# Layer 1's projections ahead of its attention, and one PSUM bank for a head's scores and transposes

## The chip, the cores and the metric

One core of a Trainium2 chip runs the whole program: two transformer blocks of two layers each, on 256 tokens (and 256 context tokens in the first block), width 1024, batch 1, float32. The metric is the device time of one execution in microseconds, as the median of several. Three executions of the kernel before took 2139.5, 2148.2 and 2151.42 us, so the median is 2148.2 us.

## The reference, cut to what matters

Only the attention of the first block is touched. Its layer 0 holds the MLA attention (`blocked_attention`, 8 heads, 512 tokens of context and latent for queries, 256 or 512 keys). Its layer 1 is `odd_mixer`:

```python
lat = split_cols(u_lat @ w_in, ODD_SPLITS); ctx = split_cols(u_ctx @ w_in, ODD_SPLITS)
c_lat = neighbourhood_attention(q0, k0, v0, k_ctx, v_ctx, rpb)   # 8 heads of 64: softmax(q k^T * s + bias) v
kd_c = rms_norm(k of ctx);  kd_l = apply_rope(rms_norm(k));  qd_l = apply_rope(rms_norm(q))
d_lat = blocked_attention(qd_l, concat(kd_c, kd_l), concat(vd_c, vd_l), scale)   # 8 heads, 2 KV heads
y_lat = concat(c_lat, d_lat) @ w_out
```

## The kernel before, in words

A matrix product in float32 is made of three matmuls on split operands (`mm3`, lines 554 to 556): each operand is a high part and a rest. Weights come by DMA on SP's queue in groups of two 128-row tiles (`Weights.load`), ACT casts the high part (L270) and DVE or POOL subtracts for the rest (L272). `linear_tok` runs over (chunk of columns, token tile) in an order given by the caller, loads a chunk's four groups at its first tile, and hands each finished PSUM bank to `consume`. In layer 1 the weights have two pools: the common one (2 raw, 2 split buffers) and `K.px` (1 raw, 2 split); `layer1` closes `K.px` after the mixer and opens a larger one for `w_out`.

The Tile framework orders the instructions: program order is the priority, and in a simulated time line each engine takes the ready instruction of highest priority, so that later code fills holes of earlier code. On the chip each engine then runs its list in that fixed order.

PSUM has eight banks of 128x512 float32. In layers 1 to 3 `mix_banks` names them acc (2), aux (1), s (2), tp (2), po (1). In layer 0 they are g (3), s (2), tp (1), po (1), gv (1), where acc is another name of s and aux of g.

`attend` treats a pair of heads for one tile of 128 queries: six score matmuls (two heads, three steps, L710) into two banks; for each head the negated maximum on DVE (L674), exp with its sum on ACT (L676), four PE transposes of the 128x512 result (L679) into another bank, a copy to SBUF (head 0 on ACT, L684; head 1 on DVE, L682). Then the reciprocal of the sums (L698), its transpose into `rb` (L700), and 16 matmuls with v into `po` (L690). Tiles p and pt have K.np = 2 buffers each. The list `kinds` says which bank each score and each transposed tile gets. `attended` (L718, L719 and a split, L306, L307) closes four pairs of a token tile.

`l1_mixer` runs: projections of v, k, q (chunks 2, 1, 0); neighbourhood attention `na(0)` on token tile 0, whose scores get a bias by DMA on POOL's queue (L1406) and a DVE add (L1407); projections of the grouped attention (chunks 4, 3), with per-head norm and rope; `na(1)`; the transposes put off into `late` (four of k, two of q, all through the one aux bank, L1350); `gqa(0)`, `gqa(1)`. There are 16 calls of `attend`. After it comes the `w_out` product.

In layer 0 `l0_mla` calls `attend` 16 times, beside the delta rule's recurrence (`gdn_run`) for head pairs 0 and 1 and after it for pairs 2 and 3. Rotary tables for the second block (`rope2_tables`) use DVE and ACT inside layer 1's attention.

Of the kernel before, what the change touches and what calls it, by code (L numbers as in the profile page):

```python
# [163 lines left out]
def closed(K, p):  # L164
    for q, cm in K.open:
        if q is p:
            cm.__exit__(None, None, None)
# [32 lines left out]
def bank(K, kind):  # L200
    kind = K.alias.get(kind, kind)
    return K.ps[kind].tile([128, 512], F32, name=nm(K, kind), tag=kind, bufs=K.kinds[kind])
# [459 lines left out]

def attend(K, score, v, po, rb, c, kinds=("s", "s", "tp", "tp")):


    nc = K.nc
    sm = cut(K, [128, 2], F32, "sm", 4)
    pts = []  # L670
    for hh, ps in enumerate(score([bank(K, kinds[0]), bank(K, kinds[1])])):
        n = ps.shape[-1]
        nmx = cut(K, [128, 1], F32, "nmx", 6)
        nc.vector.tensor_reduce(nmx, ps, axis=AX.X, op=ALU.max, negate=True)  # L674
        p = cut(K, [128, 512], F32, "p", K.np)
        nc.scalar.activation(p[:, :n], ps, AF.Exp, bias=nmx, accum_out=sm[:, hh:hh + 1])  # L676
        tp = bank(K, kinds[2 + hh])
        for j in range(n // 128):
            nc.tensor.transpose(tp[:, j * 128:(j + 1) * 128], p[:, j * 128:(j + 1) * 128], K.ident)  # L679
        pt = cut(K, [128, 512], F32, "pt", K.np)  # L680
        if hh:
            nc.vector.tensor_copy(pt[:, :n], tp[:, :n])  # L682
        else:
            nc.scalar.copy(pt[:, :n], tp[:, :n])  # L684
        pts.append((pt, n // 128))
    sums_row(K, sm.unsqueeze(1), rb, c)
    nj = pts[0][1]
    for j in range(nj):
        for hh in range(2):
            nc.tensor.matmul(po[hh * 64:hh * 64 + 64, c:c + 128], v(hh, j), pts[hh][0][:, j * 128:(j + 1) * 128],  # L690
                             start=(j == 0), stop=(j == nj - 1))
# [96 lines left out]
def l0_mla(K, O):  # L788

    nc = K.nc  # L790
# [7 lines left out]
    for t in range(4):  # L798
        n = vt[:, t, :]
# [17 lines left out]
    for k in range(4):  # L817
        ps = acc(K)
# [7 lines left out]
        g = K.col("mla_qn")[:, k:k + 1] if k < 2 else K.col("mla_kvn")  # L826
# [6 lines left out]
    for t in range(4):  # L833
        ps = acc(K)
# [4 lines left out]
    for pair in range(4):  # L839
        heads = {}  # L840
        for h in (2 * pair, 2 * pair + 1):
            if h % 4 == 0:
                wq = WQ.load(K.ins["w_q"], 0, 2, (h // 4) * 512, 512)
            late = "g" if pair >= 2 else None
            ps = bank(K, late or "acc")
            hs = slice((h % 4) * 128, (h % 4 + 1) * 128)
            for k in range(2):
                mm3(K, ps, wq[0][:, k, hs], wq[1][:, k, hs], qh[:, k, :], ql[:, k, :], k == 0, k == 1)
            u = cut(K, [128, 512], F32, "p", K.np)
            nc.vector.tensor_tensor(u, ps, K.c("qtab"), op=ALU.mult)  # L850
            q1, q2 = cut(K, [128, 512], FR, "q1", 2), cut(K, [128, 512], FR, "q2", 2)
            split(K, q1, q2, u)
            ps = bank(K, late or "acc")
            hs = slice(h * 64, (h + 1) * 64)
            mm3(K, ps[:64, :], wkh[:, 0, hs], wkl[:, 0, hs], ch, cl, True, True)
            k1, k2 = kh[h % 2], kl[h % 2]
            nc.scalar.copy(k1[:64, :], ps[:64, :])
            nc.vector.tensor_tensor(k2[:64, :], ps[:64, :], k1.bitcast(F32)[:64, :], op=ALU.subtract)
            heads[h] = (q1, q2, k1, k2)
        po, rb = bank(K, "po"), bank(K, "gv")  # L860
        for t in range(4):
            n = 256 if t < 2 else 512

            def score(pss):
                tk = slice(t * 128, (t + 1) * 128)
                for hh in range(2):
                    q1, q2, k1, k2 = heads[2 * pair + hh]
                    mm3(K, pss[hh][:, :n], q1[:, tk], q2[:, tk], k1[:, :n], k2[:, :n], True, True)
                    yield pss[hh][:, :n]
            attend(K, score, lambda hh, j: vt[:, j, pair * 128 + hh * 64:pair * 128 + hh * 64 + 64], po, rb, t * 128,  # L870
                   ("s", "g", "tp", "g") if late else ("s", "s", "tp", "tp"))
        nc.scalar.copy(O[:, pair, :], rb)
        nc.vector.tensor_tensor(O[:, pair, :], po, O[:, pair, :], op=ALU.mult)

# [479 lines left out]
def l1_mixer(K, W, oh, ol):  # L1354

    nc = K.nc
    w = K.ins["w_in_odd"][0]
    xs = kts(K.uh, K.ul)
    kh, kl = cut(K, [128, 4, 512], FR), cut(K, [128, 4, 512], FR)
    qh, ql = cut(K, [128, 4, 256], FR), cut(K, [128, 4, 256], FR)  # L1360
    gkh, gkl = cut(K, [128, 2, 512], FR), cut(K, [128, 2, 512], FR)
    gqh, gql = cut(K, [128, 4, 256], FR), cut(K, [128, 4, 256], FR)
    vn, vg = cut(K, [128, 4, 512]), cut(K, [128, 4, 128])
    rt = K.c("rope_gqa").rearrange("p (t c) -> p t c", t=2)

    def tok(t):
        return slice(t * 128, (t + 1) * 128)

    def consume(ci, t, ps):
        if ci == 2:  # L1370
            nc.scalar.copy(vn[:, t, :], ps)
            return
        x = cut(K, [128, 512], F32, "lx", 3) if ci < 3 else cut(K, [128, 512 if ci == 3 else 256], F32, "lx%d" % ci, 2)
        if ci == 4:
            nc.scalar.copy(x[:, :256], ps[:, :256])
            nc.gpsimd.tensor_copy(vg[:, t, :], x[:, 128:256])
            xv = x[:, :128].rearrange("p (h d) -> p h d", h=2)
            per_head_norm(K, xv, 2, K.row("gqa_kn"))
            if t >= 2:
                rope_tok(K, xv, 2, 64, rt[:, t - 2, :64], rt[:, t - 2, 64:], nc.gpsimd, "rk")  # L1380
            kd = cut(K, [128, 2, 2, 64], F32, "lkd", 4)
            nc.vector.tensor_copy(kd, bc(xv, [128, 2, 2, 64], 2))
            late.append(lambda: pairs_T(K, kd.rearrange("p g x d -> p (g x d)"), 2, gkh, gkl, tok(t)))
            return
        nc.scalar.copy(x, ps)
        if ci == 0:
            pairs_T(K, x, 4, qh, ql, tok(t - 2), 0.125)
        elif ci == 1:
            pairs_T(K, x, 4, kh, kl, tok(t))
        else:  # L1390
            xv = x.rearrange("p (h d) -> p h d", h=8)
            per_head_norm(K, xv, 8, K.row("gqa_qn"))
            rope_tok(K, xv, 8, 64, rt[:, t - 2, :64], rt[:, t - 2, 64:], nc.gpsimd, "rq")
            late.append(lambda: pairs_T(K, x, 4, gqh, gql, tok(t - 2), 0.125))

    chunks = [(0, 512), (512, 512), (1024, 512), (1536, 512), (2048, 256)]
    late = []

    def na(t):
        po, rb = bank(K, "po"), aux(K)  # L1400
        for pair in range(4):
            def score(pss):
                out = pair_scores(K, (qh[:, pair], ql[:, pair]), (kh[:, pair], kl[:, pair]), 512, tok(t), pss)
                for hh in range(2):
                    b = cut(K, [128, 256], F32, "nab", 4)
                    nc.gpsimd.dma_start(b, K.ins["rpbx"][2 * pair + hh, t * 128:(t + 1) * 128, :])  # L1406
                    nc.vector.tensor_tensor(out[hh][:, 256:], out[hh][:, 256:], b, op=ALU.add)  # L1407
                return out
            attend(K, score, lambda hh, j: vn[:, j, pair * 128 + hh * 64:pair * 128 + hh * 64 + 64], po, rb, pair * 128,
                   ("s", "acc", "tp", "acc") if t == 1 and pair >= 1 else ("s", "s", "tp", "tp"))  # L1410
        attended(K, po, rb, oh, ol, 0, t)

    def gqa(t):
        po, rb = bank(K, "po"), aux(K)
        for pair in range(4):
            g = pair // 2

            def score(pss):
                return pair_scores(K, (gqh[:, pair], gql[:, pair]), (gkh[:, g], gkl[:, g]), 512, tok(t), pss)
            attend(K, score, lambda hh, j: vg[:, j, g * 64:g * 64 + 64], po, rb, pair * 128, ("s", "acc", "tp", "acc"))  # L1420
        attended(K, po, rb, oh, ol, 4, t)

    linear_tok(K, W, xs, w, chunks, [(2, 0), (2, 1), (2, 2), (2, 3), (1, 0), (1, 1), (1, 2), (1, 3), (0, 2), (0, 3)],
               consume)
    na(0)
    linear_tok(K, W, xs, w, chunks, [(4, t) for t in range(4)] + [(3, 2), (3, 3)], consume)
    na(1)
    for f in late:
        f()
    for t in range(2):  # L1430
        gqa(t)

# [524 lines left out]
def layer1(K, h):  # L1959
# [5 lines left out]
    with Pool(K, "l1o"):  # L1965
# [5 lines left out]
        bk = ffn_banks(K)  # L1971
        bk.__enter__()
        K.dbg("oh", oh)
        closed(K, K.px)
        W.drop()
        pa = opened(K, "a", "right")
        K.uh, K.ul = sbt(K, [128, 8, 256], FR, pool=pa), sbt(K, [128, 8, 256], FR, pool=pa)
        K.pa = pa
# [192 lines left out]
```

## Time and profile before

| | |
|---|---|
| executions, us | 2139.5, 2148.2, 2151.42 |
| profiled execution, us | 2141.66 |
| its span in the trace, us | 2139.8 |
| PE busy, DVE busy, ACT busy, us | 2003.9, 1318.1, 923.5 |
| first projection matmul of layer 1 to its first w_out matmul, us of the span | 908.2 to 1104.9 |

The span is the time from the first to the last instruction of the profiled execution; the execution itself is 1.86 us longer. A busy share is the share of a stretch in which an engine ran an instruction. The clock column of a stretch (PEclk) is the mean granted clock of TensorE as a share of 2.4 GHz: 1.00 is the full clock and 0.50 the lower level of 1.2 GHz. Layer 1's mixer is the stretch from 908 to 1105 us, layer 0's MLA attention runs from 302 to 440 us.

### The profile page before, as it was taken

The page shows a single profiled execution, that of the slowest core. Times are in us where ns is not written, and L with a number is a line of the kernel's source. Part 1 is how long each engine was busy: PE and PEld are TensorE (multiplying, and loading weights), DVE is VectorE, ACT ScalarE, POOL GpSimd, SP SyncE. Part 2 cuts the span into 40 slices and gives each one's busy share as a digit, 9 for nine tenths or more (in the row PEclk, how much of TensorE's full clock was granted, in tenths as well). Part 3 has the DMA queues.
Part 4 walks back from the last instruction along what each step waited for, and adds up shares of the span by engine and source line. Part 5 has one row for each costly group of instructions (what it writes and reads, how often), then busy time and mean ns, then how long its engine had stood idle before and what let it go on. Part 6 is the DMA issues. An engine that isn't in the chain of part 4 may idle for free.

```text
span 2139.8 us, 31171 instructions
## 1 busy us (share of the span) xinstructions
PE 2003.9 (94%) x11656; PEld 1629.7 (76%) x11656; DVE 1318.1 (62%) x2737; ACT 923.5 (43%) x1614; POOL 241.2 (11%) x312
## 2 busy tenths in 40 slices
PE   6989799899999999799798999998999999989998
PEld 3768578678878778687466888997788789868886
DVE  5666557767776744637556555574765557577644
ACT  4533444344222234434445443564554345555532
POOL 2120112301000000213101001110200021020000
PEclk9999899899999999899689999998999999989999
DMA  8344640234686633213024654521556535155662
GB/s 282 94 114 115 197 139 26 69 100 128 190 261 209 191 105 99 91 61 102 25 89 147 188 187 149 159 87 48 189 179 194 168 108 147 31 167 177 187 187 69
DMA packets 186952, 291.90 MB, mean 136 GB/s; under 512 B 28472, under 2 KB 75704, under 8 KB 186800
## 3 DMA queue, kind: packets, MB, share of 16 engines
q1 hardware_dynamic: 172720, 272.54, 40.8%
q0 software_dynamic: 5472, 16.13, 2.2%
q10 hardware_dynamic: 8608, 1.23, 0.4%
q8 instruction: 92, 1.51, 0.3%
q14 instruction: 60, 0.49, 0.1%
HBM read 281.44 MB, written 8.41 MB: 135 GB/s over the span
## 4 chain that ended last, share of the span: by engine, by line
PE 85%; DVE 6%; DMA 4%; ACT 3%; issue 2%; ACTq 0%; POOL 0%; SPq 0%; DVEq 0%; POOLq 0%
PE acc L554 19%; PE acc L556 19%; PE acc L555 19%; PE s L554 2%; PE s L555 2%; PE s L556 2%; PE po L690 2%; PE tp L891 2%; PE po L1531 1%; PE tp L1531 1%; DMA wraw<-in_w_mod_dram 1%; PE gv L373 1%; DVE wlo L272 1%; PE tp L679 1%; PE aux L729 1%
## 5 line engine op out<-in xcount | busy, mean ns | idle before, releaser
L272 DVE TENSOR_TENSOR wlo<-wraw,whi 128x512 fp32r<-128x512 f32 (+4 forms) x772 | 482.0, 669 | 293.6 <-ACT whi L270 276.6
L270 ACT CAST whi<-wraw 128x1024 fp32r<-128x1024 f32 (+4 forms) x420 | 413.4, 990 | 483.7 <-PE acc L556 200.5
L554 PE MATMUL acc<-whi,u 128*128 128x512 f32 (+3 forms) x1320 | 510.2, 389 | 17.8 <-ACT u L306 11.2
L556 PE MATMUL acc<-whi,u 128*128 128x512 f32 (+3 forms) x1320 | 507.0, 386 | 1.2 <-DVE u L307 1.2
L555 PE MATMUL acc<-wlo,u 128*128 128x512 f32 (+3 forms) x1320 | 508.1, 387 | 0.0
L554 PEld LDWEIGHTS acc<-whi,u 128*128 128x128 f32 x1320 | 252.1, 191 | 68.0 <-ACT u L306 13.7
L556 PEld LDWEIGHTS acc<-whi,u 128*128 128x128 f32 x1320 | 251.8, 191 | 51.4 <-DVE u L307 3.6
L555 PEld LDWEIGHTS acc<-wlo,u 128*128 128x128 f32 x1320 | 252.3, 191 | 48.3 <-DVE wlo L272 1.4
L554 PE MATMUL acc<-u,whi 128*128 128x512 f32 (+1 forms) x480 | 170.0, 361 | 1.8 <-ACT u L306 1.7
L556 PE MATMUL acc<-u,wlo 128*128 128x512 f32 (+1 forms) x480 | 170.0, 358 | 0.0
L555 PE MATMUL acc<-u,whi 128*128 128x512 f32 (+1 forms) x480 | 169.5, 355 | 0.2 <-DVE u L307 0.2
L272 POOL TENSOR_TENSOR wlo<-wraw,whi 128x512 fp32r<-128x512 f32 (+1 forms) x68 | 84.0, 1266 | 431.0 <-ACT whi L270 431.0
L432 DVE SCALAR_TENSOR_TENSOR msum<-mraw,u,msum 128x512 f32<-128x512 f32 x140 | 100.8, 747 | 13.7 <-DMA mraw<-in_w_mod_dram 12.7
L554 PEld LDWEIGHTS acc<-u,whi 128*128 128x128 f32 x480 | 90.1, 189 | 17.0 <-issue 2.6
L555 PEld LDWEIGHTS acc<-u,whi 128*128 128x128 f32 x480 | 90.7, 189 | 15.1 <-issue 1.7
L556 PEld LDWEIGHTS acc<-u,wlo 128*128 128x128 f32 x480 | 90.3, 189 | 15.1 <-issue 1.7
L307 DVE TENSOR_TENSOR u<-aux,u 128x512 fp32r<-128x512 f32 (+2 forms) x96 | 59.5, 632 | 40.6 <-ACT u L306 40.4
L306 ACT CAST u<-aux 128x512 fp32r<-128x512 f32 (+2 forms) x96 | 50.3, 542 | 52.4 <-PE aux L729 36.5
L554 PE MATMUL acc<-whi,dxh 128*128 128x512 f32 x176 | 69.7, 396 | 1.9 <-ACT dxh L306 1.9
L555 PE MATMUL acc<-wlo,dxh 128*128 128x512 f32 x176 | 69.6, 396 | 0.0
L556 PE MATMUL acc<-whi,dxl 128*128 128x512 f32 x176 | 68.7, 396 | 0.0
L307 DVE TENSOR_TENSOR dxl<-u,dxh 128x1024 fp32r<-128x1024 f32 x22 | 26.7, 1224 | 52.8 <-ACT dxh L306 52.8
(511 smaller groups left out, 3103.1 us busy)
## 6 DMA issues: line engine op xcount, KB each, us to landing
wraw<-in_w_up_dram SPq DMA_DIRECT2D x64, 512.0 KB, 4.0
wraw<-in_w_down_dram SPq DMA_DIRECT2D x64, 512.0 KB, 3.9
mraw<-in_w_mod_dram SPq DMA_DIRECT2D x56, 512.0 KB, 4.9
wraw<-in_w_ffn_down_dram SPq DMA_DIRECT2D x44, 512.0 KB, 3.8
wraw<-in_w_mod_dram SPq DMA_DIRECT2D x40, 512.0 KB, 5.7
wraw<-in_w_ffn_gate_dram SPq DMA_DIRECT2D x48, 256.0 KB, 3.0
wraw<-in_w_ffn_up_dram SPq DMA_DIRECT2D x48, 256.0 KB, 3.6
wraw<-in_w_ffn_gate_dram SPq DMA_DIRECT2D x20, 512.0 KB, 3.7
```

Source lines behind the costliest of these rows:

```text
L270: self.K.nc.scalar.copy(hi, raw)
L272: e.tensor_tensor(lo[:, k], raw[:, k], hi.bitcast(F32)[:, k], op=ALU.subtract)
L306: (hi_eng or nc.scalar.copy)(hi, src)
L307: nc.vector.tensor_tensor(lo, src, hi.bitcast(F32), op=ALU.subtract)
L373: nc.tensor.matmul(ps[32 * j:32 * j + 32, :], K.cl[:, g + k, :], raw[:, k, :], start=(g + k < 4), stop=(g + k >= 4))
L432: nc.vector.scalar_tensor_tensor(accs[s], raw[:, k, :], c, accs[s], op0=ALU.mult, op1=ALU.add)
L554: mm(ps, ah, bh, start=start, stop=False)
L555: mm(ps, ah, bl, start=False, stop=False)
L556: mm(ps, al, bh, start=False, stop=stop)
L690: nc.tensor.matmul(po[hh * 64:hh * 64 + 64, c:c + 128], v(hh, j), pts[hh][0][:, j * 128:(j + 1) * 128], start=(j == 0), stop=(j == nj - 1))
L891: nc.tensor.matmul(tp[:, t * 128:(t + 1) * 128], x[:, t // 2, t % 2 * 128 + j:t % 2 * 128 + j + 128], dg[j], start=(j == 0), stop=(j == 4))
L1531: nc.tensor.matmul(ps[t][:, c * 128:c * 128 + 128], yp[:, c, t * 128 + j:t * 128 + j + 128] if j < 31 else ones, dg, start=(j == 0), stop= ...
```

## The change

`attend` no longer takes separate banks for the transposes: a head's transposes go back into the bank of its scores once exp has read them, and `copies` says which engine copies each head's transposed tile. In layer 1 each call takes both banks of one kind, in the turn acc, tp, s (`unit()`), so three pairs can be under way. Neighbourhood attention copies both heads on ACT ("SS"). All projections of layer 1 run first; `K.px` is closed and its weights dropped before the attention; the attention runs in a pool of its own with six buffers of p and pt; `late` runs between `na(0)` and `na(1)`. In layer 0 the kinds become ("s", "s") for pairs 0 and 1 and ("s", "g") for pairs 2 and 3, and the bank tp is not used by `attend` any more.

```diff
-def attend(K, score, v, po, rb, c, kinds=("s", "s", "tp", "tp")):
+def attend(K, score, v, po, rb, c, kinds, copies="SV"):
-    for hh, ps in enumerate(score([bank(K, kinds[0]), bank(K, kinds[1])])):
+    bks = [bank(K, kinds[0]), bank(K, kinds[1])]
+    for hh, ps in enumerate(score(bks)):
...
-        tp = bank(K, kinds[2 + hh])
+        tp = bks[hh]
...
-        if hh:
-            nc.vector.tensor_copy(pt[:, :n], tp[:, :n])
-        else:
-            nc.scalar.copy(pt[:, :n], tp[:, :n])
+        (nc.vector.tensor_copy if copies[hh] == "V" else nc.scalar.copy)(pt[:, :n], tp[:, :n])
# l0_mla
-                   ("s", "g", "tp", "g") if late else ("s", "s", "tp", "tp"))
+                   ("s", "g") if late else ("s", "s"))
# l1_mixer: na, gqa
-                   ("s", "acc", "tp", "acc") if t == 1 and pair >= 1 else ("s", "s", "tp", "tp"))
+                   unit(), "SS")
-            attend(K, score, lambda ..., po, rb, pair * 128, ("s", "acc", "tp", "acc"))
+            attend(K, score, lambda ..., po, rb, pair * 128, unit())
-    linear_tok(K, W, xs, w, chunks, [(2, 0), ..., (0, 2), (0, 3)], consume)
-    na(0)
-    linear_tok(K, W, xs, w, chunks, [(4, t) for t in range(4)] + [(3, 2), (3, 3)], consume)
-    na(1)
-    for f in late:
-        f()
-    for t in range(2):
-        gqa(t)
+    used = [0]
+    def unit():
+        used[0] += 1
+        return [("s", "acc", "tp")[used[0] % 3]] * 2
+    linear_tok(K, W, xs, w, chunks, [(2, 0), ..., (0, 2), (0, 3),
+                                     (4, 0), (4, 1), (4, 2), (4, 3), (3, 2), (3, 3)], consume)
+    closed(K, K.px)
+    W.drop()
+    with Pool(K, "at"):
+        K.np = 6
+        na(0)
+        for f in late:
+            f()
+        na(1)
+        for t in range(2):
+            gqa(t)
+        K.np = 2
# layer1: closed(K, K.px) and W.drop() after the mixer are gone
```

## Rows read from the trace of the kernel before

**Rows 1.** Page, part 1: busy time of each engine.

```profile
PE 2003.9 (94%) x11656; PEld 1629.7 (76%) x11656; DVE 1318.1 (62%) x2737; ACT 923.5 (43%) x1614; POOL 241.2 (11%) x312
```

**Rows 2.** Windows, layer 1: length, busy (count) by engine, PE clock, DMA share, GB/s.

```profile
908.20:1012.00 103.80, 103.53 (x555) 81.90 (x556) 54.88 (x154) 43.83 (x76) 19.42 (x31) 0.99 0.27 82
1012.00:1019.30 7.30, 4.57 (x29) 2.79 (x24) 7.30 (x19) 3.04 (x7) 4.29 (x7) 0.95 0.13 50
1019.30:1032.10 12.80, 10.01 (x47) 7.13 (x48) 9.13 (x27) 5.19 (x10) 1.22 (x1) 0.50 0.03 10
1032.10:1046.00 13.90, 8.25 (x65) 5.27 (x61) 6.74 (x12) 8.33 (x16) 5.69 (x6) 0.99 0.23 76
1046.00:1083.30 37.30, 33.52 (x128) 21.42 (x127) 13.78 (x20) 10.98 (x26) 0.00 (x0) 0.50 0.00 1
1083.30:1102.00 18.70, 18.07 (x141) 12.55 (x140) 12.73 (x18) 8.54 (x21) 0.00 (x0) 0.99 0.00 1
1102.00:1104.90 2.90, 0.05 (x2) 0.02 (x1) 1.38 (x2) 2.14 (x4) 0.00 (x0) 0.84 0.51 167
```

**Rows 3.** Chain of waits in gqa: start, us, what. One pair at each clock.

```profile
1072.49 1.90 PE po L690 x16
1080.37 1.91 PE po L690 x16
...
1085.80 0.42 PE aux L700 x2
...
1087.83 0.89 PE acc L710 x3
...
1089.31 0.89 PE s L710 x3
1090.20 0.42 PE aux L700 x2
```

**Rows 4.** Chain of waits: the six scores of na(0)'s first pair.

```profile
972.96 0.66 PE s L710 x4
...
974.84 0.43 PE s L710 x2
```

**Rows 5.** Groups by shape, 908 to 1105: line, names, shapes, count, busy, mean ns, idle.

```profile
L698 DVE RECIPROCAL rs<-sm 128x128 f32<-128x128 f32 x16 | 15.2, 950 | 6.6 <-ACT p L676 6.6
...
L676 ACT ACTIVATE p<-s,nmx 128x512 f32<-128x512 f32 x21 | 14.4, 687 | 13.4 <-DVE nmx L674 12.1 <-ACT p L676 0.7 <-DVE rst L326 0.6
L674 DVE TENSOR_REDUCE nmx<-s 128x1 f32<-128x512 f32 x21 | 14.3, 681 | 3.2 <-PE s L710 3.2
...
L684 ACT COPY pt<-tp 128x512 f32<-128x512 f32 x16 | 9.3, 584 | 19.8 <-PE po L690 16.2 <-PE tp L679 3.6
...
L1407 DVE TENSOR_TENSOR s<-s,nab 128x256 f32<-128x256 f32 x13 | 5.5, 425 | 4.3 <-PE s L710 4.3
...
L676 ACT ACTIVATION_READ_ACCUMULATOR p<-s,nmx 128x1 f32 x21 | 4.1, 197 | 0.0
...
L676 ACT ACT_TABLE_LOAD x3 | 3.8, 1283 | 0.1
```

**Rows 6.** Chain of waits: first and fifth of the six `late` calls' transposes.

```profile
1042.84 0.45 PE aux L1350 x2
...
1048.62 1.10 PE aux L1350 x4
```

**Rows 7.** Time line of DVE: start, us, the instruction (a rotary table).

```profile
1012.81 2.55 DVE L1444 TENSOR_TENSOR u<-u,const_rest 128x16 f32<-128x16 f32 x1
```

**Rows 8.** Waits of SP's queue, 895 to 1125: total us, times, longest us.

```profile
SPq L276 <- PE po L690: 101.8, 2, 59.3
```

**Rows 9.** Windows, layer 0's MLA attention (columns as in rows 2).

```profile
302.00:376.00 74.00, 72.76 (x811) 59.64 (x810) 54.41 (x96) 31.23 (x76) 14.85 (x21) 1.00 0.20 64
376.00:387.50 11.50, 8.73 (x129) 7.66 (x126) 6.74 (x12) 2.84 (x7) 2.44 (x4) 0.99 0.01 1
387.50:400.60 13.10, 12.33 (x56) 10.13 (x55) 10.06 (x27) 2.40 (x4) 6.55 (x11) 0.50 0.42 131
400.60:440.00 39.40, 35.77 (x241) 25.68 (x239) 30.41 (x57) 20.33 (x52) 7.56 (x10) 1.00 0.18 64
```

**Rows 10.** Time lines of PE and ACT: one MLA head, score and copy.

```profile
348.50 0.40 PE L554 MATMUL s<-u,q 128*128 128x512 f32 x1
...
362.04 0.59 ACT L684 COPY pt<-tp 128x512 f32<-128x512 f32 x1 [3.34 <-PE tp L679]
```

More of the change, by code (lines that the diff above doesn't have):

```diff
@@ L1419, in score @@
                 return pair_scores(K, (gqh[:, pair], gql[:, pair]), (gkh[:, g], gkl[:, g]), 512, tok(t), pss)
-            attend(K, score, lambda hh, j: vg[:, j, g * 64:g * 64 + 64], po, rb, pair * 128, ("s", "acc", "tp", "acc"))
+            attend(K, score, lambda hh, j: vg[:, j, g * 64:g * 64 + 64], po, rb, pair * 128, unit())
         attended(K, po, rb, oh, ol, 4, t)
-    linear_tok(K, W, xs, w, chunks, [(2, 0), (2, 1), (2, 2), (2, 3), (1, 0), (1, 1), (1, 2), (1, 3), (0, 2), (0, 3)],
-               consume)
-    na(0)
-    linear_tok(K, W, xs, w, chunks, [(4, t) for t in range(4)] + [(3, 2), (3, 3)], consume)
-    na(1)
-    for f in late:
-        f()
-    for t in range(2):
-        gqa(t)
+    used = [0]
+    def unit():
+        used[0] += 1
+        return [("s", "acc", "tp")[used[0] % 3]] * 2
+    linear_tok(K, W, xs, w, chunks, [(2, 0), (2, 1), (2, 2), (2, 3), (1, 0), (1, 1), (1, 2), (1, 3), (0, 2), (0, 3),
+                                     (4, 0), (4, 1), (4, 2), (4, 3), (3, 2), (3, 3)], consume)
[10 more added lines that the diff above has]
+        K.np = 2
 def rope2_tables(K, pool):
@@ L1973, in layer1 @@
         K.dbg("oh", oh)
-        closed(K, K.px)
-        W.drop()
         pa = opened(K, "a", "right")
```

## The prediction

> **What bounds the kernel now.** I read the busy times first: PE is busy for 2003.9 us, half as long again as any other engine [rows 1], so time is won only where PE idles or runs at the lower clock. The windows over layer 1 show both [rows 2]. Up to 1012 us, with projections and na(0) mixed, PE is busy 103.53 of 103.80 us at full clock. Then it breaks: 7.3 us in which DVE is busy throughout and PE for 4.57, 12.8 us at 1.2 GHz, 13.9 us at full clock but with PE busy only 8.25, 37.3 us at 1.2 GHz with PE busy 33.52, and at last 18.7 us of gqa at full clock, PE busy 18.07. The last 2.9 us are the hand-over to w_out.
>
> The chain of waits prices a pair in gqa, from one like instruction to the next [rows 3]: 1080.37 - 1072.49 = 7.88 us at 1.2 GHz, 1090.20 - 1085.80 = 4.40 us at full clock. The clock alone makes a pair 1.79 times as long; work done at the lower clock is worth 4.40 / 7.88 = 0.558 of its time.
>
> So the 196.7 us from 908.2 to 1104.9 hold this much full-clock work [rows 2]: 103.53 + 4.57 + 8.25 + 18.07 + 0.05 + 0.558 x (10.01 + 33.52) = 158.8 us. The other 37.9 us are 0.442 x 43.53 = 19.2 us of low clock and 196.7 - 178.0 = 18.7 us of idle PE, of which 2.9 are the hand-over.
>
> **The change, part by part.**
>
> *Projections first.* No matmul is added or removed; six token tiles move ahead of na(0), with their weight loads on SP's queue. They need no more DMA than before, and in the mixed stretch the same loads left PE 0.27 us idle [rows 2]. The joins of the short chunks now come without attention to fill them. A join costs between nothing (as in that stretch) and the 4.57-of-7.3 kind of gap, 2.7 us; I take 1 us for all. The attention loses its cover in return: it now stands alone, so everything below goes to PE directly.
>
> *The low clock.* It fell after stretches with PE about 60% busy and holes in it (1012 to 1019, 1032 to 1046), and it held in the 18.7 us of dense gqa [rows 2]. Removing the causes should keep it: -19.2 us, with ends 0 and -19.2. Against this I charge one excursion like that at 1019, 0.442 x 10.01 = +4.4 us, because the rotary tables and the query norm come free as the projections end and will again meet the first attention pairs: one such DVE operation took 2.55 us [rows 7].
>
> *The idle holes, 15.8 us without the hand-over.* The `late` transposes go through one aux bank, six in turn, the first five from 1042.84 to 1049.72 us, with PE mostly waiting [rows 6]. Between na(0) and na(1) the scores of three pairs of na(1) can run beside them. What is late then is `rb` of na(1), which waits for the same aux bank; its 16 po matmuls don't wait for it, and only the third pair's reciprocal (two buffers) would. New idle: joins 1; entry into the attention 3 (one head's add, maximum and exp, 0.425 + 0.681 + 0.687 + 0.197 = 2.0 us [rows 5], behind leftover norms); three table loads of 1.28 us each on ACT [rows 5], 3 of 3.8; the one po bank at three token-tile borders, 1 us each, 3. Sum 10, so -5.8 us. The ends are 6 (half of entry and tables hidden, borders 2) and 18, that is -9.8 and +2.2.
>
> *Is PE still the slowest engine?* A na pair costs DVE 2 x 0.425 + 2 x 0.681 + 0.950 = 3.16 us, since "SS" moves a copy to ACT, and ACT 2 x (0.687 + 0.197) + 2 x 0.584 = 2.94 us [rows 5]. Both are under 4.40. Six buffers of p and pt cover three pairs in flight, which is what three kinds of bank allow. So one bank per head, held from score to copy, costs nothing here: about 4 us of hold (scores 0.89, the 2.0 above, transposes 0.6, copy 0.58) against three pairs of 4.40 us. Without that cover (two pairs in flight, 8.8 us) it would still hold.
>
> *Scores side by side.* In gqa a head's three score matmuls run after the other head's: 0.89 + 0.89 = 1.78 us [rows 3]. na(0)'s first pair, with both banks free, took 0.66 + 0.43 = 1.09 us for all six [rows 4]. Three pairs in the trace run so. With both banks of one kind coming free together, up to 13 more can: 13 x 0.69 = 9.0 us. They come free one copy (0.58 us) apart, so some will not; I take half, -4.5 us, ends 0 and -9.0.
>
> *Bias loads and w_out.* The 16 bias DMAs keep their number and POOL's queue; four buffers are two pairs ahead, 8.8 us. SP waited up to 59.3 us for attention buffers before its w_out loads [rows 8], and the new pool lies in the same place: nothing changes, within 3 us either way.
>
> *Layer 0.* MLA pairs 0 and 1 now hold both s banks from score to copy. One such head took 348.50 to 362.63 us [rows 10], and before, the next scores could start after exp. PE is filled to 98% from 302 to 376 by all that runs there [rows 9], so slower attention there moves work past 376. After it PE has 2.8 us idle and 13.1 us at the lower clock, until the recurrence ends near 400: a place that takes such work, and may keep the clock up, worth 0.442 x 12.33 = 5.4 us. Ends: -5 us (work fills this stretch), and +12: eight units of at most 14.1 us one after another take 113 us instead of 74, 39 more, less the 24.6 us to 400.6, less a few us of work already in it. I take +3, nearer the lower end since half of the units have 256 keys.
>
> **Sum.** -19.2 + 4.4 - 5.8 - 4.5 + 3 = -22.1 us. The profiled execution took 2141.66 us (span 2139.8), so the same one would take 2119.6. That execution lies 6.5 us below the median of 2148.2; on the median I predict 2126 us.
>
> **A rule against it.** The Trainium skill ("TensorE: Matmul & The Clock Gate", Part 4: PE-mode transpose) says that the full clock "doesn't engage for transpose-mode". By it attention alone, with eight transposes a pair, would run at the lower clock, and the sum would be that of rival A below. The trace bears it out for 37.3 us of busy attention at 0.50 and speaks against it in the next 18.7 us at 0.99 [rows 2].
>
> **Rivals.**
>
> *A, slower: the clock falls at the entry and stays down.* All 16 pairs now run alone. At 7.88 instead of 4.40 us they cost 16 x 3.48 = 55.7 us more than full-clock work: 158.8 + 55.7 + 10 + 2.9 = 227.4 us for the stretch, less 9 for scores side by side, is 22 more than 196.7. With layer 0's 3: about 2173 us. It decides at 26.5 / 3.48, that is 7 to 8 pairs at the lower clock. For it: 37.3 us of gqa with PE busy for 33.52 lifted it only at the end [rows 2]. Against: the clock that dense work had reached held through 18.7 us of gqa, and the attention now enters from dense projections.
>
> *B, no change: the holes move.* The entry is as bad as 1012 to 1046 was, the idle stays at 15.8 us, and the low clock lasts for 33.52 us of work: -19.2 + 14.8 - 4.5 + 3 = -5.9, 2142 us. For it: DVE's leftovers become free at the same point. Against: late's chain is no longer bare.
>
> *C, layer 0 gives it back.* +12 instead of +3: 2135 us. For it: the 14 us hold. Against: the slack behind 376.
>
> *D, more than forecast.* The clock holds throughout, scores run side by side in all pairs, idle 6: -19.2 - 9.8 - 9.0 + 3 = -35, 2113 us; with layer 0's -5, 2105.
>
> **How the numbers follow.** The forecast with its own range, 2119 to 2133, has a chance of 0.47; D 0.18; B 0.16; C 0.07; A 0.12. About 0.5%, 10.7 us, is what a measurement of this kernel can tell from no change. Below 2137.5 lie the forecast, C and D and a little of B (0.02): 0.74. Within 0.5% lies the rest of B: 0.14. Slower: 0.12, A. The range reaches from D's far end, 2105, to 2150 beyond B; it leaves out A.
>
> **What would show it.** Right: the trace has the clock near 1.00 from the first projection to w_out but for some 10 us; the stretch from first projection to first w_out matmul is 170 to 175 us, where it was 196.7; pairs of gqa cost 3.7 to 4.4 us; score matmuls of the two heads start together in some pairs; PE works on during the late transposes; the recurrence and MLA end within 5 us of 440. Wrong: a clock of 0.50 over more than half of the attention (A), DVE filled and PE waiting at the entry for 15 us and more (B), PE idle in the recurrence and MLA pairs 2 and 3 starting past 410 us (C).

## The result, and the profile after

The changed kernel takes 2125.07 us (median of 4 runs, 2119.98 to 2126.78); the kernel before, timed beside it, 2149.81 us (4 runs). The ratio is 0.9893, 95% interval 0.9872 to 0.9914: 24.7 us faster, where 2126 with a gain of 22.1 was forecast. The profiled execution has a span of 2122.8 us, 17.0 less than that of before. Medians and ratios, here and below, leave out slow executions, of which there was one (order_only, 2155.59 us).

Matmul starts in the two traces divide the 17.0 into three: up to layer 1's first projection matmul (907.82, now 926.74) +18.9; from there to the first w_out matmul (197.07, now 167.30) -29.8; behind it (1034.9, now 1028.8) -6.1. Of the outer two no more than some 9 us is the change's, as the section on layer 0 shows.

The page still has PE as the bound [rows 1]:

```profile
PE 1991.6 (94%) x11656; PEld 1626.7 (77%) x11656; DVE 1315.5 (62%) x2729; ACT 924.7 (44%) x1620; POOL 242.1 (11%) x312
```

The windows of after (length, busy and count by engine, PE clock, DMA share, GB/s), first the end of layer 0's recurrence [rows 9], then layer 1 [rows 2] and what follows it:

```profile
400.00:424.00 24.00, 21.06 (x100) 16.72 (x98) 19.24 (x50) 5.58 (x14) 10.87 (x15) 0.65 0.29 88
...
926.70:1013.00 86.30, 86.27 (x438) 70.94 (x437) 39.07 (x111) 33.22 (x54) 12.40 (x20) 0.99 0.26 80
1013.00:1017.50 4.50, 1.93 (x7) 0.96 (x6) 3.20 (x11) 2.83 (x4) 3.19 (x7) 1.00 0.69 227
1017.50:1035.40 17.90, 16.43 (x70) 11.43 (x70) 16.32 (x51) 9.13 (x22) 8.95 (x14) 0.52 0.24 67
1035.40:1056.00 20.60, 19.97 (x163) 14.05 (x163) 14.69 (x28) 15.41 (x35) 8.39 (x10) 1.00 0.14 45
1056.00:1070.00 14.00, 10.36 (x71) 7.16 (x72) 9.44 (x15) 7.54 (x19) 0.00 (x0) 1.00 0.11 40
1070.00:1091.70 21.70, 21.59 (x210) 16.91 (x210) 17.71 (x28) 12.64 (x30) 0.00 (x0) 1.00 0.00 1
1091.70:1094.00 2.30, 0.00 (x0) 0.00 (x0) 1.38 (x2) 1.58 (x3) 0.00 (x0) 1.00 0.45 134
1094.00:1112.00 18.00, 17.73 (x74) 13.89 (x75) 13.09 (x23) 10.04 (x13) 0.00 (x0) 1.00 0.73 246
```

In layer 1 there is one stretch at the lower clock, 17.9 us at the entry into the attention, in place of two with 43.5 us of busy PE. From 1035.4 on the clock is full. PE still idles 2.6 of the 4.5 us of the entry's first window and 3.6 us around the last late transposes (1056 to 1070).

The time line of PE in after (start, us, instruction, idle time before it and what ended it) shows the entry, then the late transposes [rows 6] and the first scores of gqa [rows 4]:

```profile
1013.01 1.91 PE L709 MATMUL acc<-u,u 64*128 64x512 f32 x6
1018.59 1.11 PE L681 MATMUL acc<-const_id,p 128*128 128x128 f32 x4 [3.67 <-ACT p L678]
...
1046.54 0.42 PE L1349 MATMUL aux<-const_id,lkd 128*128 128x128 f32 x2
1047.01 0.96 PE L709 MATMUL tp<-u,u 64*128 64x512 f32 x3
...
1055.92 0.44 PE L1349 MATMUL aux<-const_id,lkd 128*128 128x128 f32 x2
1056.29 0.65 PE L689 MATMUL po<-pt,u 128*64 128x128 f32 x6
1057.37 0.63 PE L1349 MATMUL aux<-const_id,lx 128*128 128x128 f32 x4 [0.43 <-DVE u L307]
1058.69 0.73 PE L709 MATMUL s<-u,u 64*128 64x512 f32 x4 [0.69 <-ACT u L652]
1059.26 0.62 PE L709 MATMUL acc<-u,u 64*128 64x512 f32 x4
1059.72 0.62 PE L709 MATMUL tp<-u,u 64*128 64x512 f32 x4
```

A group of four score matmuls takes 0.62 to 0.73 us, as in before's na(0): the two heads run side by side. Elsewhere three of one head take 0.96 (1047.01), one head after the other. While the first four late transposes go through the aux bank, PE has pairs of na(1).

The chain of waits (start, us, what) at the entry and in gqa [rows 3]:

```profile
1013.06 3.40 DMA nab<-in_rpbx_dram
...
1016.55 0.43 DVE acc L1406
...
1089.70 1.91 PE po L689 x30
```

Eight gqa pairs take from 1058.69 to the last po at 1091.61: 32.9 / 8 = 4.1 us a pair, all at full clock.

### The profile page after: what moved, and what is told of

Read it like the earlier page. It is cut to its first block, busy times and chain, and to the rows that moved or that the text cites. A ratio compares the mean times of both kernels' runs of the same rounds, so it can differ in the third digit from the quotient of the medians.

```text
span 2122.8 us, 31144 instructions
## 1 busy us (share of the span) xinstructions
PE 1991.6 (94%) x11656; PEld 1626.7 (77%) x11656; DVE 1315.5 (62%) x2729; ACT 924.7 (44%) x1620; POOL 242.1 (11%) x312
## 3 DMA queue, kind: packets, MB, share of 16 engines
q1 hardware_dynamic: 172720, 272.54, 41.2%
## 4 chain that ended last, share of the span: by engine, by line
PE 85%; DVE 5%; DMA 4%; ACT 3%; issue 2%; POOL 1%; SPq 0%; ACTq 0%; DVEq 0%; POOLq 0%
PE acc L554 19%; PE acc L556 19%; PE acc L555 19%; PE s L554 3%; PE s L555 2%; PE s L556 2%; PE po L689 2%; PE tp L890 2%; PE po L1540 1%; PE tp L1540 1%; DMA wraw<-in_w_mod_dram 1%; PE gv L373 1%; PE aux L728 1%; PE aux L489 1%; PE g L1199 1%
## 5 line engine op out<-in xcount | busy, mean ns | idle before, releaser
L554 PEld LDWEIGHTS acc<-whi,u 128*128 128x128 f32 x1320 | 251.3, 191 | 66.0 <-ACT u L306 11.6
L307 DVE TENSOR_TENSOR u<-aux,u 128x512 fp32r<-128x512 f32 (+2 forms) x96 | 59.5, 632 | 41.0 <-ACT u L306 40.8
```

The source lines that it names most:

```text
L307: nc.vector.tensor_tensor(lo, src, hi.bitcast(F32), op=ALU.subtract)
L554: mm(ps, ah, bh, start=start, stop=False)
```

## The experiments

All ratios are to the kernel before in the same session, with 95% intervals. Of each kernel's layer 1, from first projection matmul to first w_out matmul, the table gives the length, PE's idle time, its busy time at the lower clock (busy time times (1 - clock) / 0.5, in steps of half a microsecond), and full-clock work: busy time less 0.442 of the part at the lower clock, by the factor of the prediction. The four columns are of one trace each. In mla_tp and after_early layer 1 is early_bias's own: 162.4, 164.2 and 163.6, so 1.8 us lie between executions of the same code.

| kernel | median us | ratio | length | idle | low clock | work |
|---|---|---|---|---|---|---|
| before | | 1 | 197.1 | 18.7 | 46.3 | 157.9 |
| after | 2125.1 | 0.9893 (0.9872 to 0.9914) | 167.3 | 10.8 | 18.2 | 148.5 |
| l0_only | 2154.7 | 1.0040 (1.0023 to 1.0057) | 195.5 | 16.5 | 47.1 | 158.2 |
| l1_only | 2120.5 | 0.9885 (0.9856 to 0.9914) | 169.9 | 11.2 | 21.2 | 149.3 |
| order_only | 2130.7 | 0.9928 (0.9899 to 0.9958) | 178.7 | 13.4 | 20.3 | 156.4 |
| banks_only | 2144.5 | 0.9994 (0.9970 to 1.0018) | 193.3 | 19.1 | 46.9 | 153.4 |
| late_last | 2133.1 | 0.9936 (0.9916 to 0.9957) | 183.1 | 14.8 | 33.5 | 153.4 |
| two_buffers | 2129.6 | 0.9923 (0.9905 to 0.9942) | 172.5 | 12.9 | 13.1 | 153.8 |
| na_sv | 2124.8 | 0.9891 (0.9874 to 0.9909) | 168.8 | 13.5 | 14.6 | 148.8 |
| early_bias | 2111.9 | 0.9848 (0.9829 to 0.9867) | 163.6 | 11.5 | 10.6 | 147.5 |
| bridge | 2113.8 | 0.9859 (0.9834 to 0.9885) | 161.8 | 9.9 | 8.6 | 148.0 |
| sin_late | 2113.6 | 0.9855 (0.9830 to 0.9881) | 162.0 | 11.0 | 11.1 | 146.1 |
| mla_tp | 2118.7 | 0.9872 (0.9841 to 0.9903) | 162.4 | 12.0 | 6.9 | 147.4 |
| after_early | 2118.8 | 0.9888 (0.9861 to 0.9915) | 164.2 | 11.6 | 11.1 | 147.8 |

### Which part of the change carries it

**order_only**: the new order, pool and six buffers; separate banks for scores and transposes and a copy on DVE, as before, but with the kinds that before has in gqa for every pair (five of its eight pairs in na have s, s, tp, tp). The same in gqa.

```diff
-                   unit(), "SS")
+                   ("s", "acc", "tp", "acc"))
```

> Layer 1's projections ahead of the attention, its own pool and six buffers, but scores and transposes in separate banks with one copy on DVE, as before; layer 0 as before. Theory (the order alone brings the clock back: -19.2 of low clock and most of the holes; one bank per head adds the side-by-side scores, some 3 to 5 us): 2121 to 2128 us, the stretch 170 to 174 us, mean granted clock of the gqa pairs 1.00. Rival (the banks carry the gain, as they let three pairs be in flight): 2135 to 2143, the clock in gqa again near 0.5 to 0.8.

**banks_only**: before's order and buffers, one bank per head in layer 1 and na's copies on ACT. The same kinds in gqa.

```diff
-                   ("s", "acc", "tp", "acc") if t == 1 and pair >= 1 else ("s", "s", "tp", "tp"))
+                   unit(), "SS")
```

> Layer 1's order of before (attention of the first row block between the projections, two buffers), but each head has one bank from the rotation and the na copies are on ScalarE; layer 0 as before. Theory (the clock falls at the late transposes as before, since these still stand alone between the attention blocks): 2143 to 2150 us, a stretch of 190 to 196 us, granted clock 0.5 to 0.6 for some 35 us behind the late transposes. Rival (one bank per head is what brings the clock back): 2122 to 2130, clock 1.00 there.

The order alone shortens layer 1 by 18.4 us and the banks alone by 3.8; together (l1_only, below) it is 27.2, some 5 more than the sum. The columns say what each does. The order takes 26 us off the busy time at the lower clock (0.442 x 26 = 11.5 us) and 5.3 off the idle time, but only 1.5 off the work. The banks take 4.5 off the work and leave idle and clock as they were in sum. So the theory on order_only was right on the clock (1.00 from 1030 to the end) and wrong in size: 178.7 is over its 170 to 174, and 2130.7 us lies between its 2121 to 2128 and the rival's 2135 and more.

The theory on banks_only held in time and stretch, but not in where the clock falls. Two windows of its trace (columns as above), and then PE's time line just ahead of the first of them:

```profile
989.00:1016.50 27.50, 27.50 (x105) 17.86 (x105) 12.07 (x20) 10.04 (x25) 3.90 (x8) 0.50 0.13 39
...
1061.00:1081.00 20.00, 14.58 (x63) 9.43 (x63) 9.94 (x17) 8.53 (x19) 4.91 (x5) 0.59 0.07 27
```

```profile
981.45 0.73 PE L708 MATMUL acc<-u,u 64*128 64x512 f32 x4 [1.25 <-ACT u L652]
982.02 0.63 PE L708 MATMUL tp<-u,u 64*128 64x512 f32 x4
982.49 0.63 PE L708 MATMUL s<-u,u 64*128 64x512 f32 x4
...
987.31 0.66 PE L680 MATMUL acc<-const_id,p 128*128 128x128 f32 x4 [2.71 <-ACT p L677]
```

Behind the late transposes the lower clock lasts for some 17 us (20 us at 0.59), not 35. Another 27.5 us lie in the stretch of na(0) and projections, which before ran at full clock: three pairs' scores go out at once there, one of them into the acc banks that the projections use too, and PE then waits 2.71 us for the exponentials. That the sum is before's is not shown to be more than chance, and what the banks do in the old order, where they meet the projections, is not what they do in the new one. So the 5 us over the sum is not shown to be the two parts helping each other.

The time line of PE in order_only shows what is missing there, the scores of one head after the other's:

```profile
1082.17 1.09 PE L689 MATMUL po<-pt,u 128*64 128x128 f32 x16
1083.19 0.66 PE L681 MATMUL acc<-const_id,p 128*128 128x128 f32 x4
1083.78 0.96 PE L709 MATMUL acc<-u,u 64*128 64x512 f32 x3
1084.67 0.66 PE L681 MATMUL tp<-const_id,p 128*128 128x128 f32 x4
...
1086.68 0.66 PE L681 MATMUL acc<-const_id,p 128*128 128x128 f32 x4
1087.27 0.96 PE L709 MATMUL acc<-u,u 64*128 64x512 f32 x3
```

Summed over the stretch (each matmul from the end of the one ahead, time at the lower clock times 0.558), the 96 score matmuls cost 26.0 us in before, 27.7 in order_only, 22.6 in banks_only and 21.0 in after. Some of order_only's 27.7 is its own: its pairs in na have lost the two s banks that let scores of two heads run together in before.

**late_last**: l1_only with the late transposes behind na(1) again.

```diff
-        for f in late:
-            f()
         na(1)
+        for f in late:
+            f()
```

> l1_only with the late transposes behind the second neighbourhood block again (projections still ahead of all attention). Theory (between the blocks the late transposes have pairs beside them, at the end the gqa scores wait for their splits): the 10 us hole of before and its fall of the clock come back, a stretch of 178 to 190 us in place of 169.9, 2129 to 2140 us. Rival (with all projections done long before and free banks the place doesn't matter): 168 to 172, 2119 to 2123.

As the theory had it: 183.1 us. The time line of PE in late_last has nothing beside the transposes:

```profile
1045.93 0.44 PE L1349 MATMUL aux<-const_id,lkd 128*128 128x128 f32 x2
1047.30 0.44 PE L1349 MATMUL aux<-const_id,lkd 128*128 128x128 f32 x2 [0.92 <-DVE u L307]
1048.66 0.44 PE L1349 MATMUL aux<-const_id,lkd 128*128 128x128 f32 x2 [0.92 <-DVE u L307]
1050.02 0.44 PE L1349 MATMUL aux<-const_id,lkd 128*128 128x128 f32 x2 [0.92 <-DVE u L307]
1051.47 1.09 PE L1349 MATMUL aux<-const_id,lx 128*128 128x128 f32 x4 [1.01 <-DVE u L307]
1053.24 1.22 PE L709 MATMUL s<-u,u 64*128 64x512 f32 x4 [0.69 <-ACT u L652]
```

and its windows behind them a lower clock again:

```profile
1048.00:1056.00 8.00, 4.72 (x20) 2.93 (x20) 2.14 (x5) 1.49 (x4) 0.00 (x0) 0.67 0.12 44
1056.00:1064.00 8.00, 6.34 (x29) 4.07 (x27) 6.15 (x10) 5.60 (x15) 0.00 (x0) 0.71 0.00 0
1064.00:1072.00 8.00, 8.00 (x45) 5.60 (x45) 4.55 (x7) 1.80 (x5) 0.00 (x0) 0.76 0.00 0
```

The place of the late transposes between the two blocks is worth 13.2 of l1_only's 27.2 us.

**two_buffers** and **na_sv**, both on l1_only:

```diff
-        K.np = 6
+        K.np = 2
```

> l1_only with two buffers of the exponentials and of their transposes in the attention, in place of six. Theory (with one bank per head three pairs are in flight, and two buffers hold back the third's exponentials): a stretch of 175 to 182 us in place of 169.9, 2126 to 2133 us. Rival (the order of PE's work sets the pace, the buffers are free in time): 169 to 172, 2120 to 2123.

```diff
-                   unit(), "SS")
+                   unit())
```

> l1_only with the second head's copy of the transposes on DVE in the neighbourhood attention too (as in the other attentions), in place of both on ScalarE. Theory (DVE has the bias adds and maxima there, ScalarE two table loads in late pairs; neither ends a pair's chain by much): a stretch within 2 us of 169.9, 2118 to 2123 us. Rival (DVE becomes the bound of the pairs): 3 to 5 us longer, 2124 to 2126.

Two buffers make the stretch 2.6 us longer, between the two forecasts; the scores cost 24.2 us again in place of 21.2, so the buffers help pairs to start together. The whole time rose by more (0.0038, and the intervals overlap), which the trace doesn't explain. For the copies' engine no difference is shown: na_sv's stretch of 168.8 us is the theory's, its 2124.8 us lie in the rival's range, but its ratio differs from l1_only's by 0.0006.

### The entry

**early_bias**: l1_only, with four bias tiles of the outer pool loaded ahead of the projections.

```diff
+    home, early = K.cur, []
+    def bias(t, head):
+        b = sbt(K, [128, 256], F32, "nab", 4, home)
+        nc.gpsimd.dma_start(b, K.ins["rpbx"][head, t * 128:(t + 1) * 128, :])
+        return b
+    early += [bias(0, head) for head in range(4)]
...
-                    b = cut(K, [128, 256], F32, "nab", 4)
-                    nc.gpsimd.dma_start(b, K.ins["rpbx"][2 * pair + hh, t * 128:(t + 1) * 128, :])
+                    b = early.pop(0) if early else bias(t, 2 * pair + hh)
```

> The kernel with the change in layer 1 alone (l1_only, 2120.5 us), and the first four bias loads of the neighbourhood attention issued ahead of the projections, into four tiles outside the attention's pool. Theory (the hole and the clock's fall at the entry both come from these loads, which stand behind the rope on POOL: 3.4 us of idle PE at 1000 to 1012 and some 16 us at 0.50, worth 7 to 8): the stretch from the first projection matmul to the first w_out matmul falls from 169.9 to 158 to 163 us, the clock stays at 1.00 through the entry, 2108 to 2114 us. Rival 1 (the hole goes, the clock falls all the same): stretch 166 to 168, 2116 to 2119. Rival 2 (the first pair waits for something else just as long): within 2 us of l1_only.

In before the loads are written behind ten projection tiles and yet go out from 897.7 us on, ahead of all of them; in after their tiles lie in the pool that opens behind the projections. In after, the time line of POOL has the rope of the last key tile, and only then the first bias loads:

```profile
1012.66 0.46 POOL L1342 TENSOR_TENSOR lx<-rka,rkb 128x128 f32<-128x128 f32 x1
1013.06 2.18 POOL L1405 DMA_DIRECT2D nab<-in_rpbx_dram  x4
```

In early_bias they are out a hundred microseconds earlier:

```profile
907.29 2.15 POOL L1401 DMA_DIRECT2D nab<-in_rpbx_dram  x4
```

The stretch falls from 169.9 to 163.6, inside the theory's 158 to 163 but for 0.6; the time at the lower clock halves. The theory's cause fails all the same: the wait and the fall don't go. The time line of PE in early_bias:

```profile
1005.43 0.96 PE L709 MATMUL acc<-u,u 64*128 64x512 f32 x3 [0.17 <-ACT lx L1384]
1009.48 1.12 PE L681 MATMUL acc<-const_id,p 128*128 128x128 f32 x4 [3.09 <-ACT p L678]
```

The first pair still waits 3.09 us for its exponentials, now behind the query norm on DVE and ACT and a 1.28 us table load; in l1_only it waited 3.03. That second wait was there in after too, 1.57 us short of the first, as ACT's time line shows:

```profile
1014.90 1.28 ACT L678 ACT_TABLE_LOAD   x1
1017.76 0.69 ACT L678 ACTIVATE p<-acc,nmx 128x512 f32<-128x512 f32 x1 [1.57 <-DVE nmx L676]
```

So the first pair gains nothing on l1_only, and the idle time as a whole (11.5 against 11.2 us) isn't what fell. What comes sooner are the heads behind it, whose bias tiles are there: eight of the sixteen loads now go out ahead of the attention, and DVE's first four bias adds run from 986.33 to 994.36 us, beside the projections (in after from 1016.55 to 1019.88). The first six exponentials start within 5.1 us (1008.64 to 1013.77), where l1_only took 7.9 and after 7.9 (1017.76 to 1025.63). How long the lower clock then lasts differs between executions with late loads as well (13.1 us of busy PE in two_buffers' stretch, 14.6 in na_sv's). The stretch is the surer measure: 161.8 to 164.2 us in the five kernels with early loads, 167.3 to 169.9 in after, l1_only and na_sv.

**bridge**: early_bias, with na(0)'s first pair ahead of the last two projection tiles (na becomes a generator that stops behind its first pair, and the turn of the banks starts at s, since the projections use acc).

```diff
-                                     (4, 0), (4, 1), (4, 2), (4, 3), (3, 2), (3, 3)], consume)
+                                     (4, 0), (4, 1), (4, 2), (4, 3)], consume)
+    first = na(0)
+    next(first)
+    linear_tok(K, W, xs, w, chunks, [(3, 2), (3, 3)], consume)
```

> early_bias (layer 1 of the change, layer 0 as before, first bias loads early; 2111.9 us, stretch 163.6), with the first pair of the neighbourhood attention written ahead of the last two projection tiles (3,2) and (3,3), so that TensorE has these tiles while the pair's biases, maxima and exponentials run. Theory (what is left of the entry's loss, 3.9 us idle at 1002 to 1014 and some 10 us at 0.50, worth 4.7, comes from this wait): the clock stays at 1.00 through the entry, the stretch is 155 to 158 us, the time 2104 to 2107. Rival 1 (the hole goes, the clock falls all the same, as the pairs behind it keep TensorE no busier): 159 to 161, 2107 to 2110. Rival 2 (the hole only moves to the second pair): 162 to 165, 2110 to 2114.

The theory fell; rival 2's mechanism is what happened, a little cheaper (161.8 us, not 162 to 165). The time line of PE in bridge has the wait at the next pair:

```profile
1012.90 0.89 PE L709 MATMUL acc<-u,u 64*128 64x512 f32 x3
1015.92 1.05 PE L681 MATMUL acc<-const_id,p 128*128 128x128 f32 x4 [2.13 <-ACT p L678]
```

and the clock falls behind it for another 6.2 us of busy PE (the table's 8.6 have 2.5 at the start of the projections). Against early_bias the stretch is 1.9 us shorter, about what executions of one code differ by, and the time is the same.

**sin_late**: early_bias, with the scratch of layer 2's rope tables in another pool, so that the two Sin activations run in the FFN.

```diff
-        k, r = cut(K, [128, 2, 8]), cut(K, [128, 2, 8])
+        k, r = sbt(K, [128, 2, 8], pool=K.cur), sbt(K, [128, 2, 8], pool=K.cur)
```

> early_bias with the scratch tiles of the rope tables of layer 2 in the pool of the moment, so that their two Sin activations fall into the FFN and no more between the exponentials of the attention. Theory (each change of table costs ScalarE 1.28 us, two of them in the attention, and ScalarE is what the pairs wait for at 1024 to 1030): stretch 160 to 162.5 in place of 163.6, 2108 to 2111 us. Rival (TensorE has other pairs beside the loads): 163 to 165, 2111 to 2114.

162.0 us is inside the theory's range but only 0.4 from mla_tp, which has the loads; the time, 2113.6, is the rival's. The trace has one table load in the stretch where early_bias has three. A gain is not shown.

### Layer 0

**l0_only** and **l1_only** divide the change by layer (MLA's kinds of bank alone, and all but these).

```diff
-                   ("s", "g", "tp", "g") if late else ("s", "s", "tp", "tp"))
+                   ("s", "g") if late else ("s", "s"))
```

> Only layer 0's MLA heads put their transposes into their own score bank; layer 1 is that of before. Theory (the change costs layer 0 some us, because a pair can no more have its second bank's transposes beside the next pair's scores): 3 to 8 us slower than before, 2153 to 2158 us by before's median of 2149.8, and the interval from the first MLA score matmul to the gdn_out projection is 3 to 8 us longer than in a kernel with four kinds of bank. Rival (the 18.5 us that the trace of after shows in layer 0 are differences between executions): within 2 us of before, 2148 to 2152. Rival C of the prediction: +12 us, 2162.

> All of the change but layer 0's MLA banks, which are those of before. Theory: layer 1 keeps its 29 us or so and layer 0 gives nothing back: 2117 to 2122 us, 3 to 8 us below after's 2125.1; the stretch from the first projection matmul to the first w_out matmul 166 to 169 us. Rival (layer 0 costs nothing): 2124 to 2126 us.

Alone, layer 0's part makes the kernel slower by 0.40% (0.23 to 0.57), 8.6 us, and that is shown. l1_only is 4.6 us under after by the medians of two sessions and 1.7 by the ratios, and its stretch 0.9 over the forecast; its ratio's interval covers after's.

The trace of after overstates the price. The recurrence's first L1211 product on gvn (L1210 in after) starts at 285.60 us there and at 275.07 in before, though the instructions up to it are the same and in the same order on every engine. Over the fourteen traces that start lies anywhere from 275.1 to 285.6: 276.8 in after_early, which has after's layer 0, 281.4 in bridge, which has before's. So 10.5 of the 18.9 us came ahead of any changed instruction. The part behind the stretch is no better: 1028.5 to 1036.3 over the traces.

From that product to the transposes just ahead of layer 1's first projection the ten kernels with the old MLA banks take 629.3 to 636.6 us (mean 632.9), the three with one bank 638.0 (l0_only), 637.7 (after) and 635.3 (after_early, below): 4.1 us more in the mean. Part of it is the clock: PE is busy at the lower clock for 19.7 to 32.3 us of that interval, whatever the kernel, and with that taken out by the table's factor 2.8 us are left. Inside it one thing is regular, the first MLA pair. In ACT's time line before has the first exponentials of its first two pairs at

```profile
304.83 0.47 ACT L676 ACTIVATE p<-s,nmx 128x256 f32<-128x256 f32 x1
...
344.09 0.47 ACT L676 ACTIVATE p<-s,nmx 128x256 f32<-128x256 f32 x1
```

and after at

```profile
315.02 0.47 ACT L678 ACTIVATE p<-s,nmx 128x256 f32<-128x256 f32 x1
...
356.74 0.47 ACT L678 ACTIVATE p<-s,nmx 128x256 f32<-128x256 f32 x1 [1.76 <-DVE nmx L676]
```

39.3 against 41.7 us. Nine of the ten kernels with the old banks have 39.2 to 39.3 (two_buffers 40.8), all with one bank 41.5 to 41.7.

**mla_tp**: early_bias, with the first two pairs' heads in one s and one tp bank (and s and g later, as in after).

```diff
-                   ("s", "g", "tp", "g") if late else ("s", "s", "tp", "tp"))
+                   ("s", "g") if late else ("s", "tp"))
```

> early_bias with one bank per head in layer 0's first two MLA pairs, but the heads in two kinds of bank (s and tp) in place of two s banks, which the projections of q and k use too; the later pairs as in after (s and g). Theory (layer 0's price, 5.6 us in the traces from the first GDN state update to the first projection of layer 1, 638 against 632, comes from s banks that are held until the copy while the tp bank lies idle): this interval is 630 to 634 us, the time 2110 to 2114 us. Rival (a head that holds its bank through the exponentials costs it wherever the bank is, or the single tp bank becomes the limit): 637 to 642, 2117 to 2122.

The interval, 635.1 us, meets neither forecast. The time, 2118.7 us, is in the rival's range, though the ratio's interval overlaps early_bias's. And the first pair takes 41.2 us, so a free third bank doesn't bring it back. That speaks for the rival, a head that holds its bank, and doesn't settle it.

**after_early**: the change as it is, with early_bias's edit.

> The change as it is, layer 0's one bank per head included, with the first four bias loads ahead of the projections. Theory (the early loads give layer 1 what they gave beside the old layer 0, and layer 0's price stays): a stretch of 162 to 165 us, the interval from the first GDN state update to layer 1's first projection 637 to 640 us against 629 to 637 in the eight kernels with the old banks there, 2115 to 2120 us, a ratio to before of 0.986 to 0.989. Rival (layer 0's price is differences between executions): interval 630 to 636, 2110 to 2114 us, a ratio of 0.984 to 0.986 as early_bias has it.

2118.8 us, ratio 0.9888 (0.9861 to 0.9915), stretch 164.2. Layer 1 does what the theory says; beside early_bias's 0.9848 the whole has layer 0's price, 0.0040 again, though the two intervals just overlap; the interval in layer 0, 635.3, is the rival's. Beside after itself (0.9893) the early loads gain 0.0005, so that here no gain in the whole time is shown, only the stretch's 3.1 us. The price of layer 0 has a sign, and a size between 2 us (after against l1_only) and 9 (l0_only) that these runs don't settle.

The version that beats both kernels is early_bias: 0.9848 (0.9829 to 0.9867) of before.

## Why the prediction was right

The clock, the holes and the scores all went the way that was forecast. In the measure of the table, before against after:

| step | forecast, us | measured, us |
|---|---|---|
| low clock, less one excursion | -19.2 + 4.4 = -14.8 | 0.442 x (18.2 - 46.3) = -12.4 |
| idle PE | -5.8 | 10.8 - 18.7 = -7.9 |
| scores side by side (all work) | -4.5, end -9.0 | 148.5 - 157.9 = -9.4, scores -5.0 of it |
| layer 0 | +3, end +12 | +2 to +9 |
| sum | -22.1 | -21 to -28; the medians have -24.7 |

- **Projections first.** PE is busy 86.27 of 86.30 us, without the 1 us charged for joins.
- **Low clock.** One excursion, as charged, but longer: 16.43 us of busy PE in its window, not 10. Rival A is out: the clock fell at the entry, as A has it, but rose again and held 1.00 from 1035.4. The Trainium skill ("TensorE: Matmul & The Clock Gate", Part 4: PE-mode transpose) says that the full clock "doesn't engage" for transpose-mode; the 56 us of attention at 1.00, with 104 transposes of p among the other matmuls, don't bear that out for such a mix.
- **The signs that were named.** Besides this excursion, two of them were missed. The stretch, 167.3 us, lies under the 170 to 175. And the last po matmul of the MLA ends at 455.6 us, not within 5 us of 440, and at 445.1 if the 10.5 us that came ahead of any change are taken off. Rival B, the holes that move, is out: 10.8 us of idle PE in place of 18.7.
- **Bias loads: the step that failed.** "The 16 bias DMAs keep their number and POOL's queue" overlooked that their tiles now lie in a pool that opens behind the projections. The first four loads were issued at 1013.06 us, behind the rope, and the first pair waited 3.67 us; the entry was charged to leftovers on DVE. Both were there: the loads ended last, the leftovers I had named stood 1.57 us behind them, and are the wait of 3.09 us in early_bias. The early loads took 6.2 us off the stretch beside l1_only and 3.1 beside after.
- **Late transposes.** PE worked on during the first four, as forecast; the last two still cost part of 3.6 us. late_last shows that their new place, not the earlier projections, removed that hole.
- **Six buffers and banks.** The banks bring the scores together (banks_only -3.4 of 26.0 us, order_only none), the buffers help (two_buffers +3.0). That the work fell by 4.4 us more than the scores was not foreseen: po and projections, 1.4 and 1.6 us less by the same count, are the larger parts, without a cause shown.
- **Is PE still the slowest.** 4.1 us a pair in gqa, and in na either copy engine does.
- **w_out.** SP's longest wait for attention buffers is 44.9 us [rows 8], the hand-over 2.3 us, within the 3 us allowed.

The waits of SP's queue in after, 920 to 1115 (total us, times, longest):

```profile
SPq L276 <- PE po L689: 79.1, 2, 44.9
```

- **Layer 0.** The price was put at +3 and is 2 to 9. That work moved to the recurrence's end "may keep the clock up" is not borne out: after's 24 us from 400 to 424 have a clock of 0.65, about 17 us of them at the lower level, where before had 13.1; but the ten kernels with the old banks have anything from 7 to 20 there. The wrong sign named for C, pairs 2 and 3 past 410 us, appears in after's trace (the third pair's first exponential at 418.7 us), but without the 10.5 us that came earlier it would be 408.2: C's +12 is not borne out.

That 2126 came within 1 us of the median owes something to luck: the holes and the work gave 7 us more than forecast, the clock 2.4 less, and layer 0 took between 1 us less and 6 more.

## What to carry to other kernels

When a block of work is moved, follow what its tiles' new pool does to the DMAs: a load is issued where its tile comes free and where its queue stands, and here that put 3.4 us of bias loads on the path. When such a wait is taken away, look for the one behind it: here the first pair waited as long as with the late loads, and what came sooner, in a stretch that was 3 to 6 us shorter, were the heads after it. An order that leaves no holes shows in low clock and idle time, banks that let two heads start together in the work; and a sum over a stretch can agree while its parts have moved, as in banks_only. Before a difference in an untouched stage is explained, compare that stage in several traces of the same code: here it moved by 10 us by itself.

## What the runs showed of the hardware

A wait of 2 to 4 us at the entry was followed by the lower clock each time: 3.67 us idle and then 15.9 us of busy PE at that level in after, 3.09 and 8.4 in early_bias, 2.13 and 6.2 in bridge. Later waits of at most 1.1 us, between 1056 and 1070 in after, left the clock at 1.00 with PE busy 10.36 of 14 us. The length of the wait alone doesn't decide it: the 2.30 us without any matmul ahead of w_out in after were followed by 18 us at 1.00.
